# Layouts prepared outside the kernel in a two-layer decoder step: input transposes left out, first weight block taken row block by row block

## The chip, the cores and the metric

The kernel runs on one core of one Trainium2 chip. The core has TensorE (matrix products; its weight loads run beside them), VectorE, ScalarE, GpSimd (called POOL in the profile) and SyncE (SP), which here only issues DMAs. The metric is the device time of one execution in microseconds; the lower the better. Three runs of the kernel before took 2745.02 to 2747.47 us, the median is 2746.14 us.

## The reference

A decoder step of two layers over 256 prompt tokens and 64 sample tokens (8 sequences of 8), width 2048, everything in fp32. Layer 0 mixes tokens by a chunked gated MLP, layer 1 by attention over 64 selected keys, with paged caches for the samples; each layer ends in a ConvFFN. Cut to its core:

```python
def _chunk_mlp(h, ...):                      # layer 0
    z = gelu(h @ w_in);  u, v = z[..., :2048], z[..., 2048:]
    v = rmsnorm(v, v_gain)
    s = einsum('gts,bnsgd->bntgd', tril(w_s), v by chunk and group) + b_s
    return (u * s) @ w_out, v
def _dsa(h, ...):                            # layer 1
    q, k, v, iq, ik, iw = split(h @ w_in);   q, k = rope(rmsnorm(q)), rope(rmsnorm(k))
    score = sum over heads of relu(iq . ik) * iw       # ik also from cache_idx_k
    sel = top_k(score, 64)
    return softmax(q . k[sel]) @ v[sel] @ w_o          # k, v also from cache_k, cache_v
def _conv_ffn(h, conv_buf, ...):             # after each mixer
    a = h @ w_in;  ap = concat(conv_buf, a)
    c = conv_b + sum_j conv_w[j] * ap[:, j:j + t]
    return (silu(c[..., :5632]) * c[..., 5632:]) @ w_out, ap[:, t:]
# x += mixer(rmsnorm(x));  x += conv_ffn(rmsnorm(x))   for both layers
```

It returns y of both groups, the new keys, values and indexer keys, the normalised v rows and the last rows of each ConvFFN.

## The kernel before

Activations lie with features on the partitions: `xT` is 16 tiles of 128 features x 320 tokens (256 prompt, 64 sample). Every fp32 operand of a large product is split into a rounded part and a remainder: activations into `hh` and `hl` (or `rh` and `rl`), weights into `wh` and `wl`. A product of a 128x128 weight tile with 320 tokens is then three TensorE instructions: `wh` with `hh`, `wh` with `hl`, `wl` with `hh` (lines 1268 to 1270). They go to the PSUM tiles called `mm`; everything else of TensorE, transposes and small products, goes to the two PSUM tiles called `sd`.

All weights stream once. `groups` lists the products: 512 output columns each (128 for one), with the input range and a function for the result. A group is cut into blocks ("units") of 1 MB, four 128-row blocks of 512 columns, loaded by `dma` into one of three `raw` buffers. Each block is split in two halves by `split`: ScalarE writes `wh`, VectorE writes `wl`, each 128x1024, into one of three buffers. The loop at line 1244 splits half n + 2, then issues the 24 products of half n. The block after next but one is loaded once a block's second half is split, so SP waits mostly for VectorE.

Between the products stand side tasks, Python generators that `Side.pump` advances after every second weight tile (six products). A task's step is emitted when an estimate of the engines' clocks, made from prices in the code, says that what it reads is ready and the queues of VectorE and ScalarE are short; a product that needs a result not yet emitted (`S.ensure`) pumps until it is there. That decides the order on each engine when the program is built; on the chip every engine takes its instructions in that order.

The side tasks that matter here:

- `x_tile` (393): x comes in token by token, 3 transposes per tile of 128 features, a copy to `xT`, then `norm_tile` (318): ScalarE `hh` and the square, VectorE `hl`, POOL adds the square to `acc`. After tile 15 `norm_fin` makes 1/rms (`rs`): a product with `ones`, a chain of small VectorE operations (`rsqrt`), a product with a diagonal matrix.
- `ws_prep` (408): the 16 mask-weight matrices of layer 0, cut to their lower triangle by POOL, transposed on TensorE; a selection product spreads 8x8 corners for the samples.
- `f_prep` (544) and `conv_out` (564): conv weights and state in, 20 transposes of 88 columns, and the last rows out, 18 transposes, per layer.
- `index_cache` (986) and `attn_sample` (1088): indexer keys (16 pages, copied twice side by side by POOL) and cached keys (8 pages for each of 8 tasks) are loaded by page number and transposed.
- `final` (625): four tiles of y are transposed back, copied and stored by three DMAs.

Gains arrive as 80 rows and are transposed at the start (1235). The first weight block is loaded in two column halves.

Of the kernel before, what the change touches and what calls it, by code (L numbers as in the profile page):

```python
# [14 lines left out]
D = 2048  # L15
# [116 lines left out]
class Engine:  # L132
    """An engine whose instructions are counted in the side work's estimate."""
# [41 lines left out]
def trunk(ctx: ExitStack, tc: tile.TileContext, i, o):  # L175
# [165 lines left out]
    # ---------------------------------------------------------------- weight stream  # L341
# [21 lines left out]
    # ================================================================ layer 0: chunked gMLP  # L363
# [3 lines left out]
    ws_raw = arena[:, ca.off:ca.off + 2048].rearrange("p (g s) -> p g s", s=128)  # L367
    wsS = ca(16, 64)
    gbc = ca(512)
    cvo = ca(512)  # L370
    bs_flat = ca(2048)
# [6 lines left out]
    v_flat = v_tok.rearrange("p a b -> p (a b)")  # L378
    xin = [v_flat[:, 1536 * b:1536 * (b + 1)].rearrange("p (a b) -> p a b", b=512) for b in range(4)]
    g_raw = zt[0][0:80, 0:128]  # L380
    sel8 = inn[1][0:8, 0:64]
    mbb = inn[1][0:64, 64:72]
    x_time = {}

    def x_load(f, n):
        c = slice(128 * f, 128 * (f + n))
        t = xin[f // 4][:, :, 128 * (f % 4):128 * (f % 4 + n)]
        sp.dma_start(t[:, 0:2, :], i["x_prompt"][:, c].rearrange("(a p) c -> p a c", p=128))
        sp.dma_start(t[0:64, 2, :], i["x_sample"][:, c])
        for k in range(f, f + n):  # L390
            x_time[k] = S.load["dma"] + 2.2

    def x_tile(f):
# [12 lines left out]
        yield from norm_tile(0, f, xT[:, f])  # L406

    def ws_prep():
        yield from wait(("rs", 0))
        sp.dma_start(ws_raw, i["a_w_s"].rearrange("g t s -> t g s"))  # L410
        sp.dma_start(bs_flat, i["a_b_s"].rearrange("g t -> (g t)").partition_broadcast(128))
        sp.dma_start(sel8, i["c_sel8"])
        sp.dma_start(mbb, i["c_mbb"])
        yield 1
        pool.affine_select(out=ws_raw, in_=ws_raw, pattern=[[0, 16], [-1, 128]], compare_op=ALU.is_ge, fill=0.0,
                           base=0, channel_multiplier=1)
        yield PE
        for q in range(4):
            ps = sd()
            for g in range(4):  # L420
# [3 lines left out]
        ps = sd()  # L424
        pe.matmul(ps[0:64, 0:128].rearrange("p (g j) -> p g j", j=8), lhsT=sel8, rhs=wsT[0:8, :, 0:8], start=True, stop=True)
        for b in range(8):
            dve.tensor_scalar(wsS[0:64, :, 8 * b:8 * b + 8], ps[0:64, 0:128].rearrange("p (g j) -> p g j", j=8),
                              mbb[:, b:b + 1], None, op0=ALU.mult)
# [101 lines left out]
    # ================================================================ ConvFFN  # L530
# [7 lines left out]
    cot = [cf(4, 128) for _ in range(2)]  # L538
    st_raw = cf(16, 128)
    cw_raw = cf(4, 128)  # L540
    cwT = cf(4, 88)
    yo = [cf(512) for _ in range(3)]

    def f_prep(l):
        sp.dma_start(cw_raw[0:88, 0:3], i["f_conv_w"][l].rearrange("j (t c) -> t j c", c=128))
        sp.dma_start(cw_raw[0:88, 3], i["f_conv_b"][l].rearrange("(t c) -> t c", c=128))
        sp.dma_start(st_raw[0:88], i["state_ffn_conv"][l].rearrange("r (t c) -> t r c", c=128))
        for a in aext:
            dve.memset(a, 0.0)
        yield PE  # L550
        ps = sd()
        for j in range(4):
            pe.transpose(ps[:, j * 88:(j + 1) * 88], cw_raw[0:88, j, :], ident[0:88, 0:88])
        dve.tensor_copy(cwT, ps[:, 0:352].rearrange("p (j t) -> p j t", t=88))
        yield PE
        for q in range(4):
            ps = sd()
            for j in range(4):
# [805 lines left out]
```

## Time and profile before

| | |
|---|---|
| median of three runs | 2746.14 us |
| the profiled execution: span from first to last instruction | 2744.7 us |
| TensorE busy | 2725.2 us, 99% |
| TensorE weight loads busy (beside the products) | 2689.4 us, 98% |
| VectorE busy | 1613.1 us, 59% |
| ScalarE busy | 1128.2 us, 41% |
| POOL busy | 145.2 us, 5% |
| DMA queue of SP | 402.44 MB, 45.5% of 16 engines |
| moved over the span | 147 GB/s |

The profile is of one execution; for what lies outside its span it shows nothing, so its own time is taken as the span, 2744.7 us. Nearly all instructions bear the line number 149, that of the helper that counts them; rows are told apart by the tiles they write and read. A product's row shows 0.31 us, but products are pipelined: the pitch from start to start is the time that each takes from TensorE.

### The profile page before, as it was taken

What the parts mean: (1) busy time and instruction counts of PE and PEld (TensorE: products, weight loads), DVE (VectorE), ACT (ScalarE), POOL (GpSimd) and SP (SyncE); (2) the same over time, 40 slices, a digit from 0 to 9 for tenths busy, and PEclk for the clock granted to TensorE, in tenths of its full rate; (3) what the DMA queues carried; (4) which work ended last, traced back from release to release, by engine and by line L of the source; (5) the groups of instructions that cost most, each with busy time, mean ns of one, the idle gap of its engine ahead of it and who ended that gap; (6) DMA issues with size and microseconds to landing.
All of it is one profiled execution on the core that took longest, in us unless ns stands there. A gap on an engine that the chain in (4) does not pass through costs nothing.

```text
span 2744.7 us, 45533 instructions
## 1 busy us (share of the span) xinstructions
PE 2725.2 (99%) x18678; PEld 2689.4 (98%) x18678; DVE 1613.1 (59%) x2852; ACT 1128.2 (41%) x1566; POOL 145.2 (5%) x378
## 2 busy tenths in 40 slices
PE   8999999999999999999999999999999999999999
PEld 7999999999999999999999999999999999999999
DVE  5465576646555654556658666766556645654653
ACT  5433344434433443444333444454334424433442
POOL 2000000101000100000000000001001000100000
PEclk9999999999999999999999999999999999999999
DMA  6443454444444444444543544354444444444443
GB/s 208 139 154 127 145 158 148 144 153 154 148 146 153 154 148 146 153 154 151 162 125 122 159 123 139 116 153 153 154 148 146 153 154 147 145 154 154 146 158 116
DMA packets 229320, 405.35 MB, mean 148 GB/s; under 512 B 12360, under 2 KB 41144, under 8 KB 228984
## 3 DMA queue, kind: packets, MB, share of 16 engines
q1 hardware_dynamic: 229112, 402.44, 45.5%
q8 instruction: 147, 2.41, 0.4%
q14 instruction: 61, 0.50, 0.1%
HBM read 396.25 MB, written 6.16 MB: 147 GB/s over the span
## 4 chain that ended last, share of the span: by engine, by line
PE 99%; ACT 0%; DMA 0%; DVE 0%; SPq 0%; issue 0%; POOL 0%; ACTq 0%; POOLq 0%; DVEq 0%
PE mm L149 93%; PE sd L149 6%; DMA arena<-x_prompt 0%; DVE wl L149 0%; SPq L149 0%; ACT wh L149 0%; DVE hl L149 0%; ACT arena L149 0%; DMA scr<-cache_idx_k 0%; ACT scr L149 0%; ACT hh L149 0%; ACT xT L149 0%; POOL scr L149 0%; DVE arena L149 0%; DVE xT L149 0%
## 5 line engine op out<-in xcount | busy, mean ns | idle before, releaser
L149 DVE TENSOR_TENSOR wl<-raw,wh 128x1024 fp32r<-128x1024 f32 x722 | 883.6, 1224 | 864.7 <-ACT wh L149 861.5
L149 ACT ACTIVATE wh<-raw 128x1024 fp32r<-128x1024 f32 x722 | 764.4, 1059 | 1218.9 <-PE mm L149 1041.5
L149 PE MATMUL mm<-hh,wh 128*128 128x320 f32 x3856 | 1206.9, 313 | 0.0
L149 PE MATMUL mm<-hl,wh 128*128 128x320 f32 x3856 | 1193.0, 309 | 1.4 <-DVE hl L149 1.4
L149 PE MATMUL mm<-hh,wl 128*128 128x320 f32 x3856 | 1192.8, 309 | 0.2 <-DVE wl L149 0.2
L149 PEld LDWEIGHTS mm<-hh,wh 128*128 128x128 f32 x3856 | 727.2, 189 | 4.5 <-issue 1.2
L149 PEld LDWEIGHTS mm<-hl,wh 128*128 128x128 f32 x3856 | 727.4, 189 | 2.1 <-DVE hl L149 1.9
L149 PEld LDWEIGHTS mm<-hh,wl 128*128 128x128 f32 x3856 | 727.0, 189 | 0.6 <-DVE wl L149 0.6
L149 PE MATMUL mm<-rh,wh 128*128 128x320 f32 x1920 | 600.0, 312 | 0.0
L149 PE MATMUL mm<-rh,wl 128*128 128x320 f32 x1920 | 594.1, 309 | 0.0
L149 PE MATMUL mm<-rl,wh 128*128 128x320 f32 x1920 | 593.9, 309 | 0.0
L149 PEld LDWEIGHTS mm<-rh,wh 128*128 128x128 f32 x1920 | 360.8, 188 | 0.5
L149 PEld LDWEIGHTS mm<-rl,wh 128*128 128x128 f32 x1920 | 360.9, 188 | 0.2
L149 PEld LDWEIGHTS mm<-rh,wl 128*128 128x128 f32 x1920 | 360.7, 188 | 0.0
L149 ACT ACTIVATE arena<-arena 128x336 f32<-128x336 f32 (+4 forms) x373 | 203.4, 559 | 127.1 <-DVE arena L149 121.8
L149 POOL COPY arena<-arena 128x16 f32<-128x16 f32 (+1 forms) x352 | 125.6, 394 | 2319.1 <-DVE arena L149 1518.3
L149 DVE SCALAR_TENSOR_TENSOR arena<-arena 128x336 f32<-128x336 f32 (+2 forms) x412 | 207.0, 507 | 8.3
L149 PE MATMUL sd<-arena 128*128 128x128 f32 (+12 forms) x1158 | 172.4, 286 | 11.8 <-DMA arena<-x_prompt 5.4
L149 PEld LDWEIGHTS sd<-arena 128*128 128x128 f32 (+7 forms) x1158 | 137.2, 160 | 36.1 <-issue 15.5
L149 DVE TENSOR_TENSOR xT<-mm,xT 128x320 f32<-128x320 f32 x240 | 115.9, 487 | 81.1 <-PE mm L149 80.7
L149 DVE TENSOR_TENSOR arena<-mm,arena 128x64 f32<-128x64 f32 (+2 forms) x417 | 127.5, 344 | 51.8 <-PE mm L149 51.6
L149 DVE TENSOR_TENSOR arena<-arena 128x256 f32<-128x256 f32 (+7 forms) x364 | 131.8, 391 | 17.1 <-DMA arena<-a_v_norm 8.4
(42 smaller groups left out, 498.2 us busy)
## 6 DMA issues: line engine op xcount, KB each, us to landing
raw<-f_w_in SPq DMA_DIRECT2D x176, 1024.0 KB
raw<-f_w_out SPq DMA_DIRECT2D x88, 1024.0 KB
raw<-b_w_in SPq DMA_DIRECT2D x33, 1024.0 KB
raw<-a_w_in SPq DMA_DIRECT2D x31, 1024.0 KB
raw<-a_w_out SPq DMA_DIRECT2D x16, 1024.0 KB
raw<-b_w_o SPq DMA_DIRECT2D x16, 1024.0 KB
arena<-cache_k SPq DMA_DIRECT2D x64, 64.0 KB
arena<-cache_v SPq DMA_DIRECT2D x64, 64.0 KB
```

The source lines that it names most:

```text
L149: return f(*a, **k)
```

## The change

Host code hands over x, the conv weights and state, the cached keys and indexer keys, the mask weights and the gains in the layout that the kernel computes in (features or head dimensions first), and turns y and the conv rows back after the kernel. On the chip the transposes of these arrays, their PSUM copies and the identity's early load are gone. Keys go to two buffers `KT` instead of one raw and one transposed buffer. `x_tile` writes `hh` and `hl` in its first step; the order of ScalarE's and VectorE's instructions changes with that. The first weight block is loaded in four row blocks, split row block by row block, and its products go row block by row block over all four output columns. Five products of `ones` with `ones` stand at TensorE's start. The diff, cut to its core:

```diff
     def x_load(f, n):
-        c = slice(128 * f, 128 * (f + n))
-        t = xin[f // 4][:, :, 128 * (f % 4):128 * (f % 4 + n)]
-        sp.dma_start(t[:, 0:2, :], i["x_prompt"][:, c].rearrange("(a p) c -> p a c", p=128))
-        sp.dma_start(t[0:64, 2, :], i["x_sample"][:, c])
+        sp.dma_start(xT[:, f:f + n], i["xT"][:, f:f + n])
...
     def x_tile(f):
-        x = xin[f // 4]
-        S.cur.t = x_time[f]
-        yield PE
-        ps = sd()
-        for tt in range(3):
-            w = TOKW[tt]
-            pe.transpose(ps[:, tt * 128:tt * 128 + w], x[0:w, tt, (f % 4) * 128:(f % 4) * 128 + 128], ident[0:w, 0:w])
-        if f % 2:
-            copy_act(xT[:, f], ps[:, 0:NT])
-        else:
-            dve.tensor_copy(xT[:, f], ps[:, 0:NT])
-        yield 1
-        yield from norm_tile(0, f, xT[:, f])
+        g = gT[:, f:f + 1]
+        if f > 3:
+            S.cur.t = x_time[f]
+            yield 1
+        act.activation(hh[:, f], xT[:, f], AF.Copy, scale=g)
+        dve.scalar_tensor_tensor(hl[:, f], xT[:, f], g, hh[:, f].bitcast(F32), op0=ALU.mult, op1=ALU.subtract)
+        S.set(("h", 0, f))
+        yield 1
+        q = yield from square_acc(("n", 0), xT[:, f], acc)
+        yield 1
+        add_acc(acc, q, pool)
...
     def ws_prep():
-        sp.dma_start(ws_raw, i["a_w_s"].rearrange("g t s -> t g s"))
+        sp.dma_start(wsT, i["a_w_sT"])
...
-                pe.transpose(ps[:, g * 128:(g + 1) * 128], ws_raw[:, 4 * q + g, :], ident)
-            copy_act(wsT[:, 4 * q:4 * q + 4, :], ps.rearrange("p (g t) -> p g t", t=128))
...
+            dve.tensor_tensor(wsS[0:64, :, 8 * b:8 * b + 8], ws8[0:64], m8x8[0:64, b:b + 1, :].to_broadcast([64, 16, 8]),
+                              op=ALU.mult)
...
     def f_prep(l):
+        sp.dma_start(cwT, i["f_convT"][l])
+        sp.dma_start(stT, i["stateT"][l])
...
-            pe.transpose(ps[:, j * 88:(j + 1) * 88], cw_raw[0:88, j, :], ident[0:88, 0:88])
...
-                pe.transpose(ps[:, j * 88:(j + 1) * 88], st_raw[0:88, 4 * q + j, :], ident[0:88, 0:88])
...
     def conv_out(l):
-                pe.transpose(ps[0:88, j * 128:(j + 1) * 128], coll[:, 4 * q + j, :], ident)
-            copy_act(t[0:88, 0:n], ps[0:88, 0:n * 128].rearrange("p (j c) -> p j c", c=128))
...
+        sp.dma_start(o["new_convT"][l], coll)
...
     def final(f):
-                pe.transpose(ps[0:w, j * 128:(j + 1) * 128], xT[:, 4 * q + j, tt * 128:tt * 128 + w], ident)
...
-            sp.dma_start(dst[:, 512 * q:512 * q + 512], t[0:w])
+        sp.dma_start(o["yT"][:, f], xT[:, f])
...
     def index_cache():
-                sp.dma_start(kd[:, j, 0:64], src)
...
-            pool.tensor_copy(kd[:, :, 64:128], kd[:, :, 0:64])
...
-                pe.transpose(ps[:, j * 128:(j + 1) * 128], kd[:, j, :], ident)
-            copy_act(ikcT(pr), ps)
+                src = i["cache_ikT"][bass.ds(pages[4 * pr + j], 1)].rearrange("a d t -> (a d) t")
+                sp.dma_start(ikcT(pr)[:, j * 128:(j + 1) * 128], src)
...
     def attn_sample(gi, hf):
-        yield from take("Kr")
+        kb = yield from take("KT", 2)
+        KT = KTs[kb]
         for j in range(8):
-            sp.dma_start(Kr[:, j], i["cache_k"][bass.ds(pages[8 * hf + j], 1), :, vc].rearrange("a p d -> (a p) d"))
-        yield PE
-        yield from take("KT")
-        for k in range(2):
-            ps = sd()
-            for j in range(4):
-                pe.transpose(ps[:, j * 128:(j + 1) * 128], Kr[:, 4 * k + j], ident)
-            copy_act(KT[:, k * 512:(k + 1) * 512], ps)
-            yield PE
-        give("Kr", 0)
+            sp.dma_start(KT[:, j * 128:(j + 1) * 128], i["cache_kT"][bass.ds(pages[8 * hf + j], 1), vc, :].rearrange("a d t -> (a d) t"))
...
-        give("KT", 0)
+        give("KT", kb)
...
     def split(n):
...
+        if un == 0:
+            for k in range(2):
+                S.ensure(("h", 0, 2 * j + k))
+                act.activation(h[:, k], src[:, k], AF.Copy)
+                dve.tensor_tensor(l[:, k], src[:, k], h[:, k].bitcast(F32), op=ALU.subtract)
...
-    sp.dma_start(g_raw, i["gains"])
-    sp.dma_start(ident, i["c_ident"])
-    x_load(0, 2)
-    dma(0, ((0, 256),))
+    pool.memset(ones, 1.0)
+    sp.dma_start(gT, i["gT"])
+    x_load(0, 1)
+    dma(0, ((0, 1),))
+    x_load(1, 1)
+    dma(0, ((1, 2),))
     x_load(2, 2)
-    dma(0, ((256, 512),))
+    dma(0, ((2, 3),))
+    dma(0, ((3, 4),))
     x_load(4, 4)
     dma(1)
...
-    pe.transpose(ps[:, 0:80], g_raw, ident[0:80, 0:80])
-    dve.tensor_copy(gT, ps[:, 0:80])
+    for _ in range(5):
+        pe.matmul(ps[:, 0:128], lhsT=ones, rhs=ones, start=True, stop=True)
...
+        if un == 0:
+            todo = [(c, c, kk, 2 * j + kk) for kk in range(2) for c in range(4)]
```

The next two fences are ScalarE's first instructions, of the kernel before and then of the changed one: `hh` is the rounded x, `wh` a rounded weight half (128x1024) or row block (128x512), `arena<-xT` the square.

```order
L149 ACTIVATE arena<-arena 128x1
L149 ACTIVATE xT<-sd 128x320
L149 ACTIVATE hh<-xT,arena 128x320
L149 ACTIVATE arena<-xT 128x320
L149 ACTIVATE hh<-xT,arena 128x320
L149 ACTIVATE arena<-xT 128x320
L149 ACTIVATE xT<-sd 128x320
```

This is the changed kernel's ScalarE in the same place.

```order
L149 ACTIVATE hh<-xT,arena 128x320 x2
L149 ACTIVATE wh<-raw 128x512 x2
L149 ACTIVATE arena<-xT 128x320 x2
L149 ACTIVATE hh<-xT,arena 128x320
L149 ACTIVATE wh<-raw 128x512
L149 ACTIVATE arena<-xT 128x320
L149 ACTIVATE hh<-xT,arena 128x320
L149 ACTIVATE wh<-raw 128x512
L149 ACTIVATE wh<-raw 128x1024
L149 ACTIVATE arena<-xT 128x320
L149 ACTIVATE wh<-raw 128x1024
L149 ACTIVATE hh<-xT,arena 128x320 x4
```

The copies from PSUM are gone, the first weight row blocks stand right behind the first two `hh`, and both halves of the second block now stand ahead of `hh` 4 to 7.

On VectorE the same place before: `hl` is the remainder of x, `wl` that of the weights.

```order
L149 COPY xT<-sd 128x320
L149 SCALAR_TENSOR_TENSOR hl<-xT,arena,hh 128x320
L149 COPY xT<-sd 128x320
L149 SCALAR_TENSOR_TENSOR hl<-xT,arena,hh 128x320
L149 TENSOR_TENSOR wl<-raw,wh 128x1024
L149 SCALAR_TENSOR_TENSOR hl<-xT,arena,hh 128x320 x2
```

And VectorE in the changed kernel:

```order
L149 SCALAR_TENSOR_TENSOR hl<-xT,arena,hh 128x320 x2
L149 TENSOR_TENSOR wl<-raw,wh 128x512 x2
L149 SCALAR_TENSOR_TENSOR hl<-xT,arena,hh 128x320
L149 TENSOR_TENSOR wl<-raw,wh 128x512
L149 SCALAR_TENSOR_TENSOR hl<-xT,arena,hh 128x320
L149 TENSOR_TENSOR wl<-raw,wh 128x512
L149 TENSOR_TENSOR wl<-raw,wh 128x1024 x2
L149 SCALAR_TENSOR_TENSOR hl<-xT,arena,hh 128x320 x4
```

`hl` 4 to 7 stand behind both `wl` of the second block.

SP's queue at the program's end, before (`out_y_...` are stores of y, `raw<-f_w_out` the last weight blocks):

```order
L149 DMA raw<-f_w_out 128x4x512
L149 DMA out_y_prompt<-arena 128x512 x2
L149 DMA out_y_sample<-arena 64x512
L149 DMA out_y_prompt<-arena 128x512 x2
L149 DMA out_y_sample<-arena 64x512
```

And SP's queue at the changed kernel's end:

```order
L149 DMA raw<-f_w_out 128x4x512
L149 DMA out_yT<-xT 128x320 x3
L149 DMA raw<-f_w_out 128x4x512 x2
L149 DMA out_yT<-xT 128x320
L149 DMA raw<-f_w_out 128x4x512
L149 DMA out_yT<-xT 128x320 x3
L149 DMA raw<-f_w_out 128x4x512 x2
L149 DMA out_yT<-xT 128x320 x8
```

Each tile of y is stored by a DMA of its own straight from `xT`.

## Rows read from the trace of the kernel before

**Rows 1.** The page, part 1: busy us, share of the span, instructions of each engine.
```profile
PE 2725.2 (99%) x18678; PEld 2689.4 (98%) x18678; DVE 1613.1 (59%) x2852; ACT 1128.2 (41%) x1566; POOL 145.2 (5%) x378
```

**Rows 2.** The chain that ended last, in order: start us, us, what.
```profile
419.74 834.43 PE mm L149 x5688
```

**Rows 3.** Groups by form on TensorE: tiles, shapes, count, busy us, mean ns, idle before.
```profile
L149 PE MATMUL mm<-hh,wh 128*128 128x320 f32 x3856 | 1206.9, 313 | 0.0
...
L149 PE MATMUL mm<-rh,wh 128*128 128x320 f32 x1920 | 600.0, 312 | 0.0
...
L149 PE MATMUL sd<-arena 128*88 128x128 f32 x36 | 5.5, 272 | 0.0
...
L149 PE MATMUL sd<-arena 88*128 88x88 f32 x40 | 4.7, 239 | 0.0
```

**Rows 4.** The same chain: transposes for mask weights, conv state, keys and y.
```profile
68.67 0.44 PE sd L149 x4
...
414.92 0.31 PE sd L149 x4
...
1562.14 0.44 PE sd L149 x4
...
2698.19 0.44 PE sd L149 x4
```

**Rows 5.** TensorE's waits, whole span: who waits, for whom, us, times, longest.
```profile
PE sd L149 <- POOL scr L149: 1.3, 1, 1.3
```

**Rows 6.** Waits of TensorE and of SP's queue from 1500 to 1770 us.
```profile
PE sd L149 <- ACT arena L149: 0.7, 1, 0.7
...
SPq L149 <- PE sd L149: 17.1, 37, 3.4
```

**Rows 7.** Weight products up to 63.6 us: busy us and count by engine.
```profile
0.00:63.60 63.60, 40.81 (x240) 37.39 (x240) 1.29 (x3) 1.00 0.62 194
```

**Rows 8.** Stretches at the start; the last three columns are granted clock, DMA share, GB/s.
```profile
0.00:5.00 5.00, 0.46 (x2) 0.28 (x3) 0.31 (x2) 1.49 (x2) 0.41 (x5) 1.00 0.38 107
5.00:10.00 5.00, 2.33 (x8) 1.12 (x8) 1.04 (x2) 2.05 (x5) 0.86 (x1) 1.00 0.90 282
...
10.00:20.00 10.00, 8.35 (x29) 6.36 (x29) 5.79 (x8) 7.05 (x13) 3.61 (x3) 1.00 1.05 337
```

**Rows 9.** Groups by form on VectorE and ScalarE: busy us, mean ns, idle before.
```profile
L149 DVE TENSOR_TENSOR wl<-raw,wh 128x1024 fp32r<-128x1024 f32 x722 | 883.6, 1224 | 864.7 <-ACT wh L149 861.5 <-PE sd L149 2.8
L149 ACT ACTIVATE wh<-raw 128x1024 fp32r<-128x1024 f32 x722 | 764.4, 1059 | 1218.9 <-PE mm L149 1041.5 <-issue 173.3 <-ACT wh L149 0.8
...
L149 ACT ACTIVATE hh<-xT,arena 128x320 fp32r<-128x320 f32 x64 | 35.0, 552 | 12.5 <-DVE xT L149 12.3
```

**Rows 10.** TensorE's instructions in order: start us, us, what; in brackets idle before.
```profile
14.59 0.63 PE L149 MATMUL mm<-hh,wh 128*128 128x320 f32 x1
...
28.99 0.41 PE L149 MATMUL mm<-hl,wh 128*128 128x320 f32 x1 [1.26 <-DVE hl L149]
```

**Rows 11.** The chain at the start: two pieces with weight products.
```profile
15.71 4.64 PE mm L149 x16
...
33.51 3.72 PE mm L149 x24
```

**Rows 12.** VectorE's instructions in order: start us, us, what.
```profile
25.93 0.54 DVE L149 SCALAR_TENSOR_TENSOR hl<-xT,arena,hh 128x320 fp32r<-128x320 f32 x1
...
40.81 1.17 DVE L149 SCALAR_TENSOR_TENSOR hl<-xT,arena,hh 128x320 fp32r<-128x320 f32 x1
```

**Rows 13.** VectorE's chain behind the first norm's sum, first and last row.
```profile
51.20 0.22 DVE L149 TENSOR_SCALAR arena<-sd 128x2 f32<-128x2 f32 x2 [1.82 <-PE sd L149]
...
53.64 0.64 DVE L149 TENSOR_SCALAR arena<-arena 128x128 f32<-128x128 f32 x3
```

**Rows 14.** The end, in order: VectorE's last addition and SP's last issue.
```profile
2738.24 0.49 DVE L149 TENSOR_TENSOR xT<-mm,xT 128x320 f32<-128x320 f32 x1 [1.27 <-PE mm L149]
...
2741.18 0.47 SPq L149 DMA_DIRECT2D out_y_sample<-arena  x1
```

More of the change, by code (lines that the diff above doesn't have):

```diff
@@ L370, in trunk @@
     cvo = ca(512)
+    ws8 = cvo[:, 0:128].rearrange("p (g t) -> p g t", t=8)
+    m8x8 = cvo[:, 128:192].rearrange("p (b t) -> p b t", t=8)
     bs_flat = ca(2048)
@@ L408, in ws_prep @@
+        if cnt["h", 0] == NK:
+            S.add(norm_fin(0), 2)
     def ws_prep():
         yield from wait(("rs", 0))
-        sp.dma_start(ws_raw, i["a_w_s"].rearrange("g t s -> t g s"))
+        sp.dma_start(wsT, i["a_w_sT"])
         sp.dma_start(bs_flat, i["a_b_s"].rearrange("g t -> (g t)").partition_broadcast(128))
-        sp.dma_start(sel8, i["c_sel8"])
-        sp.dma_start(mbb, i["c_mbb"])
+        sp.dma_start(ws8[0:64], i["a_w_s8"])
+        sp.dma_start(m8x8[0:64], i["c_m8"])
         yield 1
-        pool.affine_select(out=ws_raw, in_=ws_raw, pattern=[[0, 16], [-1, 128]], compare_op=ALU.is_ge, fill=0.0,
-                           base=0, channel_multiplier=1)
@@ L417, in ws_prep @@
-        yield PE
-        for q in range(4):
-            ps = sd()
-            for g in range(4):
-                pe.transpose(ps[:, g * 128:(g + 1) * 128], ws_raw[:, 4 * q + g, :], ident)
-            copy_act(wsT[:, 4 * q:4 * q + 4, :], ps.rearrange("p (g t) -> p g t", t=128))
-            yield PE
-        ps = sd()
-        pe.matmul(ps[0:64, 0:128].rearrange("p (g j) -> p g j", j=8), lhsT=sel8, rhs=wsT[0:8, :, 0:8], start=True, stop=True)
+        pool.affine_select(out=wsT, in_=wsT, pattern=[[0, 16], [1, 128]], compare_op=ALU.is_ge, fill=0.0,
+                           base=0, channel_multiplier=-1)
@@ L625, in final @@
     def final(f):
[L626 to L643 removed]
+        sp.dma_start(o["yT"][:, f], xT[:, f])
+        yield 1
     def f_start(l):
@@ L729, in trunk @@
     cA = Carve(phase)
-    Kr = cA(8, 128)
-    KT = cA(1024)
+    KTs = [cA(1024) for _ in range(2)]
     Vr = cA(8, 128)
@@ L1210, in split @@
         S.cur = Task(None, 0, True, 0.0)
-        act.activation(h, src, AF.Copy)
-        dve.tensor_tensor(l, src, h.bitcast(F32), op=ALU.subtract)
+        if un == 0:
[3 more added lines that the diff above has]
+                dve.tensor_tensor(l[:, k], src[:, k], h[:, k].bitcast(F32), op=ALU.subtract)
+        else:
+            act.activation(h, src, AF.Copy)
+            dve.tensor_tensor(l, src, h.bitcast(F32), op=ALU.subtract)
         S.cur = None
@@ L1230, in trunk @@
     x_load(12, 4)
-    pool.memset(ones, 1.0)
+    sp.dma_start(ident, i["c_ident"])
     dve.memset(sm_v, 1.0)
@@ L1357 @@
     ins = {k: nc.dram_tensor(k, x.shape, mybir.dt.from_np(x.dtype), kind="ExternalInput").ap() for k, x in a.items()}
-    res = {k: nc.dram_tensor("out_" + k, s, F32, kind="ExternalOutput").ap() for k, (s, _) in outs.items()}
+    res = {k: nc.dram_tensor("out_" + k, s, F32, kind="ExternalOutput").ap() for k, s in outs.items()}
     with tile.TileContext(nc) as tc:
@@ L1362 @@
     r = run_bass_kernel_spmd(nc, [a], core_ids=[0]).results[0]
-    return tuple(r["out_" + k].reshape(s) for k, (_, s) in outs.items())
+    r = {k: np.asarray(r["out_" + k]) for k in outs}
+    y = r["yT"].transpose(2, 1, 0).reshape(NT, D)
+    conv = r["new_convT"].transpose(0, 2, 3, 1).reshape(2, 18, 2 * FF)
+    return (
+        y[0:SEQ].reshape(1, SEQ, D),
+        y[SEQ:].reshape(8, 8, D),
+        r["new_k_prompt"].reshape(1, 1, 2, 128, 4, 128),
+        r["new_v_prompt"].reshape(1, 1, 2, 128, 4, 128),
+        r["new_idx_k_prompt"].reshape(1, 1, 2, 128, 64),
+        r["new_k_sample"].reshape(1, 8, 8, 4, 128),
+        r["new_v_sample"].reshape(1, 8, 8, 4, 128),
+        r["new_idx_k_sample"].reshape(1, 8, 8, 64),
+        r["new_chunk_v_sample"].reshape(1, 8, 8, D),
+        conv[:, 0:2].reshape(2, 1, 2, 2 * FF),
+        conv[:, 2:].reshape(2, 8, 2, 2 * FF),
+    )
```

123 lines of the change are left out of this document (30 added, 93 removed).

## The prediction

> **What bounds the kernel now.** I read the page's busy shares first: TensorE is busy 2725.2 us of the 2744.7 us span [rows 1]. The chain of waits agrees: one stretch of 834.43 us holds 5,688 weight products and nothing else [rows 2]. That gives the unit of everything below, 834.43 / 5,688 = 0.1467 us for a product of 320 columns. The groups of TensorE instructions count 3,856 and 1,920 products of one kind, and there are three kinds: 17,328 products, 2,542.0 us [rows 3]. The other 202.7 us of the span are start, end, waits and the small side products and transposes. Since TensorE hardly waits outside the start, a side instruction taken off it shortens the span by its own pitch; whatever VectorE, ScalarE or a queue saves counts only where TensorE waits for it. So three places are worked out: the transposes in the middle, the start, the end.
>
> **Transposes in the steady stream.** The chain shows their pitch between full-pace products: four of 128 columns take 0.44 us (one of the sets for the mask weights, one for cached keys, one for y), four of 88 columns 0.31 us [rows 4]. So 0.11 and 0.077 us each. Removed: 16 in `ws_prep`; 20 per layer in `f_prep`, 40 of 88 columns; 18 per layer in `conv_out`, 36 [both counts in rows 3]; 16 in `index_cache`; 4 groups x 2 halves x 8 = 64 in `attn_sample`; in `final` 48, of which 12 belong to the end and 36 count here. That is 16 + 36 + 16 + 64 + 36 = 168 at 0.11 us, 18.5 us, and 40 at 0.077 us, 3.1 us: 21.5 us. The PSUM copies that go with them lie on ScalarE and VectorE, which TensorE does not wait for in these places, so I count them at nothing. The small selection product in `ws_prep` goes too and is not counted. The 16 loads of cached indexer keys no longer pass through POOL; TensorE's one wait for that copy, 1.3 us, goes [rows 5], and the next reader of those keys comes tens of us later. Bounds for that wait: 0 to 1.3; I take 1.3. On the queues I count nothing either: one load or store stands for several in `f_prep` and `conv_out`, 16 stores of y for 12, and the doubled indexer keys are half a MB more, beside the 1 MB of each weight block; were a block held up by that, the two in store cover 14 us (96 products).
>
> In the attention stage TensorE waits 0.7 us in one piece for ScalarE between 1500 and 1770 us [rows 6]. With 7 us of transposes gone, dependent steps stand closer together, and waits could appear. The nearest rows are that 0.7 us (a gain, if it goes) and SP's 17.1 us of waiting for TensorE in 37 pieces, the longest 3.4 us [rows 6]: if six key loads (the third to the eighth, which wait for a buffer) each held TensorE by 3.4 us, 20 us would be lost. I take 0, near the first row, because the weight stream stands up to three blocks ahead.
>
> **The start.** By 63.6 us TensorE has done 240 products [rows 7], 35.2 us at full pace: 28.4 us are lost. Now the same for the change, by walking its order with the durations of before. Bytes first: the core took in 107 GB/s in the first 5 us, 282 in the next 5, then 337 [rows 8]: 0.54, 1.95 and 5.32 MB by 5, 10 and 20 us. In the new order of SP's queue gains, x tile 0, weight row block 0, x 1 and weight block 1 end at 0.04, 0.20, 0.47, 0.63, 0.89 MB, so x 1 is there at about 5.4 us, weight block 1 at 6.3; x 2 and 3 at 1.22 MB (7.4 us), weight blocks 2 and 3 at 1.75 MB (9.3 us), x 4 to 7 at 2.40 MB, the second weight block at 3.45 MB: 10 + 1.50 / 0.337 = 14.4 us.
>
> The five products of `ones` run while TensorE has nothing else to do, so I count them at nothing, as long as they end before 6.5 us.
>
> ScalarE rounds x 0 and x 1 (`hh`, 0.55 us each [rows 9]), then the first weight row (half of the 1.06 us of a 128x1024 split, a bit more for the fixed part: 0.6): the first product starts at about 6.5 us instead of 14.59 [rows 10]. The first block needs 48 products, 7 us at full pace, 13.9 us at the pace of the first ones (0.29 us each from 15.71 on [rows 11]). Either way it meets the next obstacle: the second block's data at 14.4 us. ScalarE splits both its halves before it rounds x 4: 14.4 + 1.06 + one square of about 0.5 + 1.06 = 17.0, `hh` 4 at 17.6; VectorE makes the second `wl` until 18.2 (1.22 us [rows 9]) and `hl` 4 at 18.8, 5 to 7 at 0.54 us each [rows 12] until 20.4. The first column ends there, 36 more products take 5.3 us: the second block ends at 26.0. 96 products are 14.1 us, so 11.9 us are lost.
>
> The third block loses about 1 us on `hl` 10 and 11, because an `hl` takes 0.54 us alone but 1.17 us in the row at 40.81 [rows 12] and POOL's sums come closer together now. In the fourth, `hh` 14 and 15 stand on ScalarE behind a weight split that must wait until TensorE has left the half before: 34.2 + 1.06 + 0.55 + 0.55 = 36.4, `hl` 15 near 37.4, end near 43.0. The norm then comes later in TensorE's order than before (198 products in, not 168), so its VectorE chain, 3.1 us from 51.20 to 54.28 [rows 13], is not hidden: it runs behind a `wl` that ends at 45.3, the product with the diagonal ends at 49.2, a `wl`, the copy of `rs` and one eviction follow, and product 216 starts at 50.6. Lost by then: 50.6 - 31.7 = 18.9 us. Up to product 240 before has 0.66 us of later side products, the change 0.33. So 19.2 against 28.4, rounded: 9 us gained.
>
> Bounds: at best the second block starts as soon as its first split is done, 15.5 us, and nothing waits behind it: 15.5 - 7.0 + 1.2 for the norm = 9.7 us lost, 18 us gained. At worst the first 96 products all run at 0.29 us, ending at 6.5 + 27.8 = 34.3, 8.3 us later than I walked: 1 us gained. I take 9, from the walk, which uses rows for every step.
>
> **The end.** The last weight product is followed by VectorE's 0.49 us addition at 2738.24; then transposes, copies and three DMAs, the last issued from 2741.18 to 2741.65 [rows 14], and the span ends 3.05 us after that. Now the DMA follows the addition: 2738.73 + 0.05 + 0.47 + 3.05 = 2742.3, 2.4 us sooner. Between 1.4 (two more issues in the queue ahead of it) and 3.0 (a lone DMA lands faster).
>
> **Sum.** 21.5 + 1.3 + 0 + 9 + 2.4 = 34.2 us. Against the profiled span: 2710.5 us. The median of the runs, 2746.14 us, is 1.4 us above that span; I add it: 2712 us.
>
> **Rivals.**
> A, the gain of the start is lost. TensorE waits between the first and the second block, from about 14 to 17 us if the first runs at full pace, and could then run its next products at the slow pace again. Rows for it: the first products of before ran at 0.29 us [rows 11]. Against it: before TensorE stood idle for 1.26 us up to 28.99, behind an `hl`, and soon after 24 products took 3.72 us, 0.155 us each [rows 10, 11]. The granted clock reads 1.00 throughout the first 20 us [rows 8], though the first pitches fit the lower level of 1.2 GHz and the later ones the upper, 2.4 GHz. Price: 48 products x 0.14 us = 6.9 us, up to the 8.3 us of the bound above: 2719 to 2720 us. The Trainium skill, "TensorE: Matmul & The Clock Gate", section "HAM oscillation — how this bites in real kernels", speaks for A: a product burst shorter than the DMA wait behind it makes the engine start the next burst cold. By that rule the sum would be 2719; before's gap of 1.26 us is too short to settle it.
> B, the transposes' room is filled by waits in attention. Steps that hid behind the key transposes wait in the open: 5 to 10 us of the 7 + 1.3 come back, 2717 to 2722 us. For it: TensorE already waited once for a copy in layer 1 [rows 5]. Against: only 0.7 us in attention itself.
> C, slower. SP issues weights and keys in one queue. A key load now waits for the score product that last read its buffer, and everything behind it waits too. If a wait exceeds the two weight blocks in store, about 14 us, TensorE starves. To end slower by 0.2%, six loads would have to cost 6.6 us each, 39.7 us: over 2751 us. It decides from an SP wait of some 20 us; the longest wait for TensorE is 3.4 us.
> D, the change does less than it says: the start gains nothing and half of the removed transposes were hidden. 2744.7 - 11 - 2.4, about 2732 us. The exact pitch between full-pace products speaks against it.
>
> **How the numbers follow.** Forecast 0.72, A 0.12, B 0.09, D 0.04, C 0.03. The forecast's own spread is the start's bounds, attention and the end: 2703 to 2718. With A and B, and less than 2 in 10 left out, 2703 to 2721. A measurement of this kernel can tell a difference of about 0.2%, 5.5 us, from none; forecast, A, B and D are all faster by more. So faster 0.95; 0.03 within 0.2% and 0.02 slower, from C and its neighbourhood.
>
> **What would show it.** TensorE's count of products should reach 240 at about 54 us; the first product should start near 6.5 us, the 49th near 17 to 19 us, behind `hh` and `hl`. There should be no groups with 88 columns or 88 partitions, no wait for POOL's copy, and the attention stage should be 7 us shorter with TensorE's waits under 2 us. The last addition should be followed by a DMA and 3 to 4 us. Wrong would be: a product pitch near 0.29 us after 20 us; new waits of TensorE for keys, or of SP beyond 14 us; a start in which unit two begins after 22 us.

## The result, and the profile after

The changed kernel takes 2713.31 us (median of 4 runs, 2711.72 to 2716.11), the kernel before 2746.80 beside it (2745.02 to 2747.81): a ratio of 0.9882, 95% interval 0.9868 to 0.9896. The profiled execution spans 2711.3 us, before 2744.7. The forecast was 2712 us, 2703 to 2721.

The page's part 1 of the changed kernel answers to [rows 1]:

```profile
PE 2692.9 (99%) x18417; PEld 2663.3 (98%) x18417; DVE 1608.3 (59%) x2839; ACT 1101.9 (41%) x1510; POOL 149.0 (5%) x374
```

TensorE has 261 instructions fewer and is as full as before. Its longest piece of the chain answers to [rows 2]:

```profile
1804.90 903.08 PE mm L149 x6156
```

903.08 / 6,156 is 0.1467 us for a product, as before. So one measure serves for all that follows: the *loss* at product n is the start of weight product n, counted from 0, less n x 0.1467 us. Read off TensorE's instructions in order, it splits the 33.4 us of span (2744.68 to 2711.32):

| stretch | loss before, us | after, us | gained, us | forecast, us |
|---|---|---|---|---|
| start, to product 240 | 28.48 | 21.80 | 6.7 | 9 |
| product 240 to the last | 167.54 | 143.99 | 23.55 | 22.8 |
| last product to the end | 6.79 | 3.66 | 3.13 | 2.4 |

Product 240 and the last one, before and then after:

```profile
63.69 0.39 PE L149 MATMUL mm<-hh,wh 128*128 128x320 f32 x1
...
2737.89 0.31 PE L149 MATMUL mm<-rh,wl 128*128 128x320 f32 x1
```
```profile
57.01 0.40 PE L149 MATMUL mm<-hh,wh 128*128 128x320 f32 x1
...
2707.66 0.31 PE L149 MATMUL mm<-rh,wl 128*128 128x320 f32 x1
```

TensorE's waits in the changed kernel, whole span (who waits, for whom, us, times, longest):

```profile
PE mm L149 <- ACT wh L149: 3.6, 1, 3.6
PE mm L149 <- DVE hl L149: 3.1, 4, 1.3
PE sd L149 <- ACT scr L149: 2.2, 3, 0.7
PE mm L149 <- ACT hh L149: 1.6, 2, 1.0
PE mm L149 <- DVE arena L149: 1.5, 1, 1.5
...
PE sd L149 <- DVE rl L149: 1.0, 1, 1.0
PE sd L149 <- DVE arena L149: 0.7, 1, 0.7
```

The wait for POOL's copy of [rows 5] is gone. All but the waits for `scr`, which stood in before too, and for `rl` lie in the first 52 us. The attention has one wait of 1.0 us, for `rl`, where it had 0.7 us for ScalarE. SP's waits there, from 1500 to 1770 us, answer to [rows 6]:

```profile
SPq L149 <- DVE arena L149: 45.6, 6, 12.9
SPq L149 <- PE sd L149: 25.0, 31, 6.7
```

Those for TensorE grew, 25.0 us where 17.1 were, the longest 6.7 us instead of 3.4; SP's longest wait there is one of 12.9 us for VectorE, 10.8 before. TensorE waited for no key transfer: no DMA stands among its releasers.

The start on TensorE, in order (start us, us, what, in brackets the idle time before):

```profile
1.07 2.50 PE L149 MATMUL sd<-arena 128*128 128x128 f32 x10 [1.07 <-POOL arena L149]
7.21 0.64 PE L149 MATMUL mm<-hh,wh 128*128 128x320 f32 x1 [3.64 <-ACT wh L149]
...
10.24 0.47 PE L149 MATMUL mm<-hl,wh 128*128 128x320 f32 x1
...
10.75 0.31 PE L149 MATMUL mm<-hh,wh 128*128 128x320 f32 x1
...
17.21 0.41 PE L149 MATMUL mm<-hh,wh 128*128 128x320 f32 x1 [1.01 <-ACT hh L149]
18.97 0.42 PE L149 MATMUL mm<-hl,wh 128*128 128x320 f32 x1 [1.35 <-DVE hl L149]
```

The first row holds the five products of `ones`, two instructions each. The first weight product is at 7.21 us, 14.59 before [rows 10]. Some 12 products run 0.267 us apart, then 0.147. At 17.21 product 48 waits for `hh`. ScalarE shows why:

```profile
14.34 1.06 ACT L149 ACTIVATE wh<-raw 128x1024 fp32r<-128x1024 f32 x1 [2.98 <-DMA raw<-a_w_in]
...
15.66 1.05 ACT L149 ACTIVATE wh<-raw 128x1024 fp32r<-128x1024 f32 x1
16.61 1.91 ACT L149 ACTIVATE hh<-xT,arena 128x320 fp32r<-128x320 f32 x4
```

The four x tiles, which landed at 11.6 us, are rounded behind both splits of weights that landed at 14.3. Product 96 is at 26.05 us. Then the first norm on TensorE:

```profile
44.46 0.71 PE L149 MATMUL sd<-arena 128*128 128x1 f32 x6
...
48.72 1.04 PE L149 MATMUL sd<-arena 128*128 128x128 f32 x6 [0.70 <-DVE arena L149]
51.29 0.39 PE L149 MATMUL mm<-hh,wh 128*128 128x320 f32 x1 [1.53 <-DVE arena L149]
...
52.18 0.47 PE L149 MATMUL mm<-hl,wh 128*128 128x320 f32 x1
...
55.11 0.31 PE L149 MATMUL mm<-hh,wh 128*128 128x320 f32 x1
```

Between 51.7 and 55 us the products stand 0.267 us apart without any wait between them. This stretch gives the reason in the third last column, the granted clock:

```profile
50.00:60.00 10.00, 8.71 (x51) 8.72 (x52) 3.99 (x8) 5.82 (x15) 1.90 (x1) 0.83 0.85 319
```

0.83 is a mean over the 10 us: for a part of them TensorE had the lower of its two levels, 1.2 instead of 2.4 GHz.

The end, in order, answers to [rows 14]: stores of y are issued at 2703.24, 2705.00 and 2706.76 us, while TensorE still works, and behind the last addition there is one more store and nothing else. 2708.00 + 0.49 to 2711.3 is 2.8 us.

```profile
2708.00 0.49 DVE L149 TENSOR_TENSOR xT<-mm,xT 128x320 f32<-128x320 f32 x1 [1.27 <-PE mm L149]
...
2708.52 0.33 SPq L149 DMA_DIRECT2D out_yT<-xT  x1
```

### The profile page after: what moved, and what is told of

It is laid out like the page before. It is cut to its first block, busy times and chain, and to the rows that moved or that the text cites. A ratio compares the mean times of both kernels' runs of the same rounds, so it can differ in the third digit from the quotient of the medians.

```text
span 2711.3 us, 44873 instructions
## 1 busy us (share of the span) xinstructions
PE 2692.9 (99%) x18417; PEld 2663.3 (98%) x18417; DVE 1608.3 (59%) x2839; ACT 1101.9 (41%) x1510; POOL 149.0 (5%) x374
## 4 chain that ended last, share of the span: by engine, by line
PE 98%; DVE 1%; DMA 0%; ACT 0%; issue 0%; SPq 0%; POOL 0%; ACTq 0%; POOLq 0%
PE mm L149 93%; PE sd L149 5%; DMA raw<-a_w_in 0%; DVE wl L149 0%; SPq L149 0%; DVE arena L149 0%; ACT wh L149 0%; POOL arena L149 0%; DVE hl L149 0%; ACT scr L149 0%; ACT arena L149 0%; DVE xT L149 0%; ACT hh L149 0%; DVE rl L149 0%; ACTq L149 0%
## 5 line engine op out<-in xcount | busy, mean ns | idle before, releaser
L149 DVE TENSOR_TENSOR wl<-raw,wh 128x1024 fp32r<-128x1024 f32 (+1 forms) x724 | 886.5, 1225 | 857.8 <-ACT wh L149 857.3
L149 ACT ACTIVATE wh<-raw 128x1024 fp32r<-128x1024 f32 (+1 forms) x724 | 766.3, 1059 | 1264.4 <-PE mm L149 1081.7
L149 PE MATMUL sd<-arena 128*128 128x128 f32 (+8 forms) x961 | 142.1, 288 | 5.2 <-ACT scr L149 2.2
L149 DVE TENSOR_TENSOR arena<-arena 128x256 f32<-128x256 f32 (+9 forms) x372 | 133.6, 389 | 18.3 <-DMA arena<-a_v_norm 8.4
L149 PEld LDWEIGHTS sd<-arena 128*128 128x128 f32 (+3 forms) x961 | 115.2, 165 | 23.7 <-issue 7.9
```

Of the source, the lines that this page charges most:

```text
L149: return f(*a, **k)
```

## The experiments

**The steady term: the keys transposed on TensorE again.** The changed kernel, with the cached keys loaded as before and 64 transposes of 128 columns and 16 copies put back in `attn_sample`.

```diff
-            sp.dma_start(KT[:, j * 128:(j + 1) * 128], i["cache_kT"][...])
+            sp.dma_start(Kr[:, j], i["cache_k"][...])
+            for j in range(4):
+                pe.transpose(ps[:, j * 128:(j + 1) * 128], Kr[:, 4 * k + j], ident)
+            copy_act(KT[:, k * 512:(k + 1) * 512], ps)
```

> The changed kernel with one part undone: cached keys come token by token again and are transposed on TensorE (64 transposes, 16 copies). Theory (a side instruction costs TensorE its own pitch, because TensorE is never waiting there): 64 x 0.11 = 7.0 us more, span 2718.3 against 2711.3, all of it between products 9840 and 10800. Rival (the transposes were hidden in waits, or the room is filled by new waits): 0 to 3 us.

It took 2720.31 us (2719.19 to 2720.88), ratio to before 0.9904 (0.9888 to 0.9921). Products 9,636 and 10,800, the ends of the attention, first in the changed kernel, then in this one:

```profile
1498.28 0.42 PE L149 MATMUL mm<-hh,wh 128*128 128x320 f32 x1
...
1748.62 0.31 PE L149 MATMUL mm<-rh,wh 128*128 128x320 f32 x1
```
```profile
1497.26 0.42 PE L149 MATMUL mm<-hh,wh 128*128 128x320 f32 x1
...
1754.80 0.31 PE L149 MATMUL mm<-rh,wh 128*128 128x320 f32 x1
```

250.34 us against 257.54: 7.2 us for 64 transposes, 0.1125 each, and the medians differ by 7.0. Of the 7.2 us, 0.85 lie ahead of product 9,840, where none was expected. Nothing was hidden and nothing came back as a wait: TensorE's waits in the attention add up to 1.1 us here and to 1.0 in the changed kernel. Rival B falls, and with it D's hidden transposes. The span of this profile is only 6.2 us longer, since its start lost 1.4 us less (below).

**What in the start matters: three parts taken singly.** First, the first weight block loaded and split in column halves instead of row block by row block; its products go by columns again too, and x 0 and 1 come in one load:

```diff
-    x_load(0, 1)
-    dma(0, ((0, 1),))
-    x_load(1, 1)
-    dma(0, ((1, 2),))
+    x_load(0, 2)
+    dma(0, ((0, 256),), True)
 ...
-            src = src[:, 2 * j:2 * j + 2, :]
```

> The changed kernel, but the first weight block comes and is used in column halves again, as before the change; x still comes ready. Theory (the second block's data and the order on ScalarE and VectorE set the start): the first product moves from 7.2 to 8 or 9 us, product 96 stays at 26.0 within 0.5 us and the span within 1 us. Rival (taking the first block row block by row block is what gains the start): product 96 two or more us later, and the span too.

Its one run took 2717.65 us. The first product came at 6.98 us, and product 96 at 31.10 instead of 26.05: 5 us, where half a us at most was expected, and the rival's two or more. The other order of the steps put a second wait for `hl` into block 2 (1.98 us, after one of 1.61), and from there products ran 0.267 us apart for a while; the granted clock reads 0.66 from 20 to 30 us. The waits of block 2 add up to 4.1 us instead of 2.4, so some 1.7 of the 5 us are waits and most of the rest goes with the clock. With one run, it isn't shown that the order of the first block and not chance brought that fall: it came in block 2 in another kernel too, whose first block is as in the changed one (below).

Second, the five products of ones left out:

```diff
-    for _ in range(5):
-        pe.matmul(ps[:, 0:128], lhsT=ones, rhs=ones, start=True, stop=True)
```

> The changed kernel without the five products of ones at TensorE's start. Theory (they bring TensorE to its full pace earlier, but the first block has slack until the second block's data are there): the first block's 48 products run at 0.27 us for longer than to 10.5 us, end before 20 us instead of 16, and product 96 moves by 0 to 2 us. Rival (they have no effect on the pace): all rows as in the changed kernel, full pace from 10.5 us.

2714.64 us in its one run. The first 20 products ran at the slow pace, to 13.4 us, and product 96 came at 26.52, 0.5 us later. But with five ones that pace lasts 12 to 22 products, from profile to profile, so the ones' worth isn't shown by this. What is shown is the cover: block 2 waits for its operands, whether the first block is early or late, as the prediction had it.

Third, the squares added on VectorE instead of POOL:

```diff
-        add_acc(acc, q, pool)
+        add_acc(acc, q)
```

> The changed kernel with the 15 additions of the first norm on VectorE instead of POOL. Theory (POOL's additions hold up VectorE's hl and wl, which take 1.1 instead of 0.55 and 1.9 instead of 1.2 us beside them, and ScalarE waits for POOL before squares): hl back to 0.55 us, no waits of ScalarE for POOL, product 192 at 40 to 42.5 us instead of 43.6. Rival (VectorE is the narrower engine there, 15 x 0.49 = 7.3 us more work on it): product 192 later than 43.6.

2713.93 us in its one run, no gain, but for two opposite reasons. From product 96 to 204 the loss grew by 0.74 us, where it grew by 4.2 in the changed kernel: an `hl`, 1.17 us beside POOL's additions, is back at 0.55.

```profile
21.06 0.55 DVE L149 SCALAR_TENSOR_TENSOR hl<-xT,arena,hh 128x320 fp32r<-128x320 f32 x1
```

Before that, by product 96, it had lost 4.9 us more than the changed kernel. Two more waits, 0.87 and 0.23 us, and 0.6 us more in the first two of block 2 are part of it. The rest, some 3 us, goes with the clock, in a stretch of this kernel (third last column):

```profile
20.00:30.00 10.00, 8.91 (x38) 8.00 (x37) 6.97 (x12) 5.82 (x13) 0.00 (x0) 0.66 0.48 176
```

The Trainium skill, "SBUF — State Buffer", section "Who interferes with whom", has the rule behind the `hl`: a VectorE instruction with two inputs in that memory and a GpSimd instruction that reads it block each other. 1.17 against 0.55 us agrees.

**The clock at the norm: the waits filled.** Eight products nobody reads, two ahead of the product with the diagonal and six behind it. The kernel ran once, then four times beside the changed kernel, itself unaltered.

```diff
+        if st == 0:
+            fill(2)
         ...
         dve.tensor_copy(rs, ps[:, 0:NT])
+        if st == 0:
+            fill(6)
```

> The changed kernel with eight more products of ones with ones, whose results nobody reads: two in front of the product with the diagonal in the first norm, six behind it, in the places where TensorE waited 0.70 and 1.53 us. Nothing else moves. Theory (part of the start's missing gain is that TensorE, after those waits, runs its next products at 0.267 us, the lower of its two clocks): with the waits filled, the rows behind the norm stand at 0.147 us from the first one, and products 216 to 240 take 4.0 to 4.4 us, where they took 5.72 in the changed kernel; the loss at product 240 falls from 21.8 to about 20.5 us. Rival (products 216 to 240 are slow because something else holds them: operands, banks or evictions): they still take 5.5 us or more, and the fillers only cost up to 0.5 us. If only a part of the pitch comes back, the waits before the last one count too.

> The kernel of e5_norm_filled again, now timed. In its first profile it gained 1.7 us at the norm and lost 3.0 us near 1590 us, where the granted clock fell. Theory (that second fall was chance): products 216 to 240 take 4.0 to 4.4 us again, products 10068 to 10104 lose about 3.9 us as in the changed kernel instead of 6.8, and the median is 0.5 to 2 us below the changed kernel's. Rival (a full pace at the start brings the fall in attention): 6.8 us lost there again, and no gain in the median.

> The changed kernel once more, unchanged, as the yardstick for the two timed beside it. Theory (falls of TensorE's clock come or stay away from execution to execution and cost 1.5 to 3 us each): the runs spread over 3 us or more again, 2711 to 2716, and the stretch of products 216 to 240 differs from the 5.72 us of the first profile, anywhere from 4.0 to 7.0 us, while products 96 to 204 keep their loss of 4.2 us within 0.5. Rival (what differs between the kernels is in their instructions): 5.5 to 6.0 us again.

TensorE at the norm with the waits filled (the single run; L308 are the fillers, two instructions each):

```profile
47.72 0.61 PE L308 MATMUL sd<-arena 128*128 128x128 f32 x4
48.58 1.04 PE L149 MATMUL sd<-arena 128*128 128x128 f32 x6 [0.26 <-DVE arena L149]
49.55 1.60 PE L308 MATMUL sd<-arena 128*128 128x128 f32 x12
51.16 0.39 PE L149 MATMUL mm<-hh,wh 128*128 128x320 f32 x1
51.38 0.31 PE L149 MATMUL mm<-hl,wh 128*128 128x320 f32 x1
...
52.99 0.31 PE L149 MATMUL mm<-hh,wh 128*128 128x320 f32 x1
```

Product 216 starts when it did, 51.16 us against 51.29, and the next ones stand 0.147 apart at once. Products 216 to 240 take 4.17 us in this profile and 4.18 in that of the four runs, 5.72 in the changed kernel and 5.70 in its repeat. So the fall of the clock behind the norm cost 1.55 us, and with the waits filled it stayed away twice; that operands or banks held the products is refuted.

The whole kernel tells the rest. The single run took 2714.53 us, because the clock fell elsewhere, in the attention. Stretches of that execution:

```profile
50.00:60.00 10.00, 10.00 (x73) 9.82 (x72) 5.53 (x9) 6.57 (x16) 1.98 (x1) 1.00 0.86 319
1580.00:1590.00 10.00, 9.87 (x66) 9.51 (x65) 7.86 (x18) 4.23 (x8) 0.00 (x0) 0.90 0.42 131
1590.00:1600.00 10.00, 10.00 (x58) 9.23 (x59) 5.10 (x22) 3.36 (x10) 0.00 (x0) 0.76 0.34 115
```

Products 10,068 to 10,104 lost 6.8 us there, 5.4 in the profile of the four runs, 3.9 in both profiles of the changed kernel. So neither forecast of the four runs held: the fall came again, half as long (0.83 from 1590 to 1600 us). Timed, the filled kernel takes 2712.18 us (2711.36 to 2714.62), the changed one 2713.91 (2711.61 to 2715.90): 1.7 us less, with ranges that overlap, so no settled gain.

The repeat's runs spread over 4.3 us, as expected, but at the norm it gave the rival's number, 5.70 us. A difference does show between profiles of the same instructions: the kernel with the keys transposed again issues what the changed one does up to the attention, and there the clock fell in block 2 (0.96 and 0.86) and not at the norm:

```profile
10.00:20.00 10.00, 7.88 (x42) 7.40 (x42) 6.62 (x9) 6.79 (x13) 2.42 (x2) 0.96 1.04 399
20.00:30.00 10.00, 10.00 (x62) 10.00 (x61) 7.88 (x9) 7.47 (x16) 8.47 (x7) 0.86 0.69 236
50.00:60.00 10.00, 8.56 (x61) 8.58 (x62) 5.53 (x9) 6.29 (x16) 1.72 (x1) 1.00 0.84 318
```

**The order in the start: x tiles rounded ahead of the weights.** One run, then four.

```diff
         else:
+            if un < 4:
+                for k in range(4):
+                    S.ensure(("h", 0, 4 * un + k))
             act.activation(h, src, AF.Copy)
```

> The changed kernel with one rule more in the weight split: in blocks 2 to 4 of the first group, the four x tiles of the block are rounded (hh and hl) before its weights are split. Theory (in the changed kernel product 48 starts at 17.2 instead of 16.1 us, and its second one 1.35 us later, because hh 4 and hl 4 stand on ScalarE and VectorE behind both weight splits, though x 4 to 7 landed before the weights): product 48 starts at 16.0 to 16.4 us, as soon as TensorE is done with the first block, and product 96 at 23 to 24 instead of 26.05. Blocks 3 and 4 may lose about 1 us each on POOL's sums, as before; the loss at product 192 falls from 15.4 to 12.5 to 14 us. Rival 1 (x 4 to 7 land no sooner, the transfers set the time): product 48 stays at 17 us. Rival 2 (the wait only moves into block 3): product 96 early, product 192 still at a loss of 15 us or more.

> The kernel of e6_x_ahead again, now timed. Theory: its start is 4.5 to 6 us shorter than the changed kernel's by product 240, and nothing later undoes it: a median of 2706.5 to 2709 us beside 2712 to 2714 for the changed kernel on the same chip. Rival (its single run of 2707.66 us was a lucky one): within 2 us of the changed kernel.

2707.66 us, then 2708.35 (2707.07 to 2710.47; ratio to before 0.9852, 0.9836 to 0.9869), 5.6 us under the changed kernel's 2713.91 on the same chip. The theory named the right order and the wrong place. ScalarE and TensorE in the single run, apart:

```profile
11.44 1.92 ACT L149 ACTIVATE hh<-xT,arena 128x320 fp32r<-128x320 f32 x4
14.13 1.06 ACT L149 ACTIVATE wh<-raw 128x1024 fp32r<-128x1024 f32 x1 [0.77 <-DMA raw<-a_w_in]
```
```profile
26.40 0.42 PE L149 MATMUL mm<-hh,wl 128*128 128x320 f32 x1 [1.67 <-DVE wl L149]
...
33.31 0.70 PE L149 MATMUL sd<-arena 128*128 128x1 f32 x6
...
39.35 0.97 PE L149 MATMUL sd<-arena 128*128 128x128 f32 x6
```

x 4 to 7 are rounded by 13.4 us. Product 48 starts at 17.24, not at 16.1, since in this execution the first 22 products ran at the slow pace, not 12; block 2 then runs without a wait, and product 96 is at 24.28, 1.8 us sooner. By product 192 only 0.6 us of that are left, and nothing in the profile of the four runs (a loss of 15.84 us): the second rival's number. But two things are in it. Block 3 waits 1.67 us for `wl`, behind `hl` beside POOL's additions (2.37 in the other profile). And the norm's own small products, 1.75 us, now stand ahead of product 192: its sum at product 138 instead of 198, the product with the diagonal at 174 instead of 216. The gain is at the norm. The sum starts at 33.31 us, 6 us ahead of the product with the diagonal, not 4.3, and VectorE's chain is done in time. From product 96 to 240 the kernel loses 5.6 us where the changed one loses 9.8: the waits of 0.70 and 1.53 us and the fall of 1.55 us are gone.

**Both, and both with fillers.** The rounding ahead, with the additions on VectorE; then the same with ten products of ones instead of five and the eight fillers at the norm.

```diff
-        add_acc(acc, q, pool)
+        add_acc(acc, q)
```

> The x tiles rounded ahead of the weights as in e6_x_ahead, and the additions of the squares on VectorE instead of POOL as in e4_vector_adds. Theory (two causes that add: the order of ScalarE and VectorE costs 3 us in block 2, POOL's sums stretch hl and wl and hold the squares, 3.5 us from product 96 to 204): product 96 near 23.5 us, loss at product 204 near 10 to 11 us instead of 16.2, and the kernel 4 to 5 us faster than the changed one, 2708 to 2709 us. Rival (VectorE becomes what is waited for once it adds as well): loss at product 204 stays above 14 us, 2711 us or more. A fall of the clock after a short wait, as in e4_vector_adds, would take 2 to 3 us back in either case.

```diff
-    for _ in range(5):
+    for _ in range(10):
```

> e7_together with ten products of ones instead of five ahead of the first product, and the eight fillers at the first norm of e5_norm_filled. Theory of the clock (what TensorE did just before sets the pace of the next products): the first products leave the pace of 0.267 us sooner than in the changed kernel, where about 12 ran at it, 1.5 us; and after the norm none run at it, another 1 to 2 us. Together 1 to 3 us faster than e7_together, 2706 to 2708 us. Rival (the ones only push the first product back, and the data sets the rest): no faster than e7_together, the first product later than 7.2 us.

2708.20 us (2705.65 to 2708.96) and 2709.18 (2708.40 to 2710.95). The additions on VectorE give one more us in the start (a loss of 13.83 at product 204, 14.82 without them; 10 to 11 was expected, above 14 by the rival), which the timing doesn't show. So the time came as forecast, 2708 to 2709 us, but not by the way that was forecast. The fillers give nothing, as their rival had it: with those two waits at the norm gone there is no fall to prevent there, and from product 168 to 180 the loss grows by 2.70 us instead of 0.90. The ten ones ended 2.5 us before the first product, and this is what TensorE did then:

```profile
1.07 4.64 PE L149 MATMUL sd<-arena 128*128 128x128 f32 x20 [1.07 <-POOL arena L149]
8.18 0.42 PE L149 MATMUL mm<-hh,wh 128*128 128x320 f32 x1 [2.47 <-ACT wh L149]
8.44 0.31 PE L149 MATMUL mm<-hl,wh 128*128 128x320 f32 x1
8.91 0.56 PE L149 MATMUL mm<-hh,wl 128*128 128x320 f32 x1 [0.16 <-DVE wl L149]
9.27 0.47 PE L149 MATMUL mm<-hh,wh 128*128 128x320 f32 x1
```

The first two products ran at the full pace, the next ones 0.267 us apart: the ones had brought the clock up, and it fell all the same (a granted clock of 0.50 from 9 to 12 us).

## Why the prediction was right, and where it missed

**What bounds.** Right. TensorE's side instructions set the steady time; a transpose taken off shortens the span by its pitch. The keys put back measured 0.1125 us, the row said 0.11 [rows 4]. For the other transposes that is argued from the same pitch; they were not put back.

**Steady term.** 22.8 forecast, 23.55 measured (18.5 + 3.1 is 21.6, not 21.5, which leaves 0.65); no run separates the rest. Attention was taken at 0, with a bound of 20 us for keys that wait for a buffer. SP's waits for TensorE did grow to 6.7 us, and the weights in store covered them, so C never began.

**The end.** 2.4 forecast, 3.13 measured; the bound was 3.0, and the sign was 3 to 4 us behind the last addition. From its end to the end of the span it is 2.8 us, and the sum had 0.05 + 0.47 + 3.05 = 3.6: a store's issue and landing were taken too long.

**The start.** 9 forecast, 6.7 measured, inside the bounds of 1 to 18. The walk held far: product 96 was forecast at 26.0 us and came at 26.05, the fourth block was to end at 43.0 and product 192, its end, came at 43.58; product 216, forecast at 50.6, came at 51.29. One sum on the way is off: 20.4 + 5.3 is 25.7, not 26.0; the first column ended at 20.76 us, and that makes the difference. The 0.29 us of the slow pace is a row's length over its products, 4.64 / 16; from start to start it is 0.267. The step that failed is "Up to product 240 before has 0.66 us of later side products, the change 0.33. So 19.2". It took every product behind the norm at full pace and half of the side products. The stretch took 5.72 us: 24 products are 3.52, side products 0.65 instead of 0.33, and 1.55 the clock that fell behind the norm's waits. With the 0.7 us by which product 216 was late, that is the 2.6 us between 19.2 and 21.8. The filled waits show the 1.55; where the clock keeps up, in the kernel with the keys back, the loss at 240 is 20.40.

**The sum.** 34.2 us forecast and 33.4 measured are nearer than the parts: the start gained 2.3 us less, the steady stretch and the end 1.5 us more. That they nearly cancel is luck.

**Rival A** had the right mechanism and, for this execution, the wrong place and price. It looked for the fall between blocks 1 and 2, after the longest wait, at 7 to 8 us. It came after two waits of 0.70 and 1.53 us, and cost 1.55, since some 12 products ran slowly and not 48. With it one of the prediction's own signs of being wrong showed, a pitch near 0.29 us after 20 us. In the kernel with the keys back, whose start has the same instructions, it came in block 2, and the loss at product 96 was 13.55 us instead of 11.97: 1.6 us, most of it taken up again by the waits that follow. The Trainium skill, "TensorE: Matmul & The Clock Gate", section "HAM oscillation — how this bites in real kernels", tells of a short burst and a longer wait for a transfer. Where the prediction used it, the burst was the longer one, 9 us from 7.21 us on, and the wait 1.01 us; at the norm, too, waits shorter than the work ahead of them were enough, and the measurement decides.

**What stays open.** Why a fall comes in one execution and not in the next. It followed stretches in which TensorE stood still several times for 0.2 to 2 us or ran short side products; no row tells more. The same waits at the norm were followed by a fall in two profiles and not in a third, so they alone do not decide.

Two patterns over all profiles and runs go further than the experiments. In seven of the twelve profiles of the changed kernel and its variants the clock fell within the first 60 us, and in none of these again before the last product. In the other five it did not, and in four of them, the filled kernel's two, the timed rounding ahead and the first of the two kernels with both, it fell in the attention instead, near 1590 us, where the stretch of products 10,068 to 10,104 then lost 5.4 to 6.8 us. That a start without a fall brings that one, the rival named for the four filled runs, is so far a pattern and not shown; it would explain why the fillers brought no settled gain.

And the spread of 4.4 us in the changed kernel's runs goes with the clock. Its eight runs took 2711.61 and 2711.72 us at a mean granted clock of 1.000, 2713.01 to 2715.90 at 0.999, 2714.32 and 2716.11 at 0.998. Where the falls lay in the runs without a profile isn't known.

That the rounding ahead gains at the norm is read from its traces; the norm's place was not moved alone. Nor is it separated which part of the change gained the start's 6.7 us: x was not transposed on the chip again.

## What to carry over

Where one engine is full, count its side instructions at the pitch they have between its full-pace products, and let everything else count only where that engine waits. Walk a start step by step with measured durations, through every engine's own order, and look where a step stands behind another that it doesn't need. Then add a price for the clock at each cluster of short waits on TensorE, about 1.5 us here, since a walk that takes every product at full pace leaves it out. It is a chance and not a certainty: here the fall came in some executions and not in others, and where the waits were filled it came later.

## What the runs showed of the hardware

- Waits of 0.70 and 1.53 us with 1 us of small products between them were followed by some 12 products at 0.267 instead of 0.147 us in two profiles and by none in a third; with the waits filled, by none in two.
- The granted clock in the rows shows such a fall (0.83 over 10 us for 1.55 us lost, 0.66 without the ones, where products 216 to 240 took 6.99 us), but not the slow pace of the first products: it reads 1.00 over the first 20 us of the changed kernel, in which 12 products ran at 0.267. The trace's records of the clock begin at its first rise, at 10.7 us there and 21.1 us before, and time without a record counts as 1.00.
- How long the slow pace at the start lasts differs from profile to profile: 12 to 22 products with five ones ahead, in ten profiles, 20 without any. Ten ones, from 1.07 to 5.7 us, left the first product or two at full pace after 2.47 us of standing still; then the slow pace came, for 12.
- With the same order of loads the first product started anywhere from 6.4 to 8.2 us in the eleven profiles that load the first block row block by row block, and product 96 moved by only 0.6 us, 25.9 to 26.5, in the five with the changed kernel's order of rounding and no fall before it.
